# Weights of two attention layers split ahead, parked in DRAM and loaded as parts

## The chip, the cores and the metric

The kernel runs on one core of one Trainium2 chip. The metric is the device time of one execution in microseconds (us), lower is better; a time given is the median of several executions. TensorE (PE) does the matmuls, VectorE (DVE), ScalarE (ACT) and GpSimd (POOL) the elementwise work, SyncE (SP) issues most of the DMAs.

## What is computed

512 tokens of width 1024 pass through two blocks, all in float32. The first block has one layer, the second two. Cut to the calls:

```python
# first block
h = rms_norm(x, mix_norm_g)
u, q, k, v, f_logit, g_ssm, g_att = split(h @ w_in)
y_ssm = s5_branch(u, ...)             # val * sigmoid(gate), [val, gate] = split(gelu(y) @ w_glu)
y_att = forgetting_attention(q, k, v, f_logit, ...)      # 8 heads of 128
x = x + (sigmoid(g_ssm) * y_ssm + sigmoid(g_att) * y_att) @ w_out
x = x + peer_ffn(rms_norm(x), ...)    # product keys: 16 of 16384 experts for each of 8 heads
# second block: an even and an odd attention layer, each followed by a feed-forward
y = rmsnorm(x) @ ev_w_in              # latent, rotary, index and differential parts
x = x + concat([dsa_mixer(...), diff_mixer(...)]) @ ev_w_out    # even: top-128 keys by index scores; differential heads
x = x + (silu(h @ w_gate) * (h @ w_up)) @ w_down
y = rmsnorm(x) @ od_w_in
x = x + nsa_mixer(...) @ od_w_out     # odd: compressed, selected and window branches
x = x + (silu(h @ w_gate) * (h @ w_up)) @ w_down
out = rmsnorm(x)
```

## The kernel before

The stages follow one another: mixer of the first block (0 to about 465 us), its experts (to about 1855), the even attention layer (to 2213), a feed-forward (to 2588), the odd attention layer (to 2995), a second feed-forward and the last norm. Instructions are written in one program order; a scheduler then puts each engine's instructions in an order by when their inputs are ready on its own timeline, so work of neighbouring steps mixes. Each engine and each DMA queue then runs in that fixed order.

Every weight is used in two float32r parts: a product is three matmuls, high by high, high by low and low by high (`mm3`, L332 to L334). The class `Stream` (L57 to L98) makes the parts. All weights stand in one list, `specs`, in the order of their use, cut into units of [128, 1024] (512 KB). `_load` (L66) issues a DMA on SP into a raw tile, `wraw` (three buffers, L68). `_split` (L72) copies the raw tile on ACT into `whi` (L77) and subtracts on DVE into `wlo` (L78); `whi` and `wlo` have three buffers each. `get` (L81) is called where a unit is needed: it splits up to two units further and loads up to three further than that. A unit's `whi` and `wlo` come free when its matmuls have read them. 525 units pass through the stream.

The units differ by where they come from. `add_t` gives units that lie in DRAM as 128 rows of 4 KB; `add_256` gives four pieces of 128 rows of 1 KB (256 columns each); `add_row` two pieces of 512 columns.

The stages that the change touches:
- the gates of the first mixer (L908 to L926): eight steps `g_att`, each a unit and 24 matmuls of 512 columns (`proj_T`), a tanh and a product into `merged`; then eight steps with a unit `glu` (two products, `pv` and `pg`) and a unit `g_ssm`. Before them run the last attention heads and the state-space branch, after them `w_out`.
- the first feed-forward (`ffn` with i = 0, L1220): 22 steps with a unit `gate` and a unit `up`, silu and product, split into `ah` and `al`; then the rows of `down`.
- the even attention layer (`even_mixer`): `ev_a`, `ev_iq`, `ev_qk`, `ev_vb`, `ev_qn`, `ev_out`, 32 units. After the index scores a selection runs as background work on DVE: 16 times `max` and `match_replace` (L1448, L1449) for each of three row tiles, handed out between the differential heads; the latent attention needs its result.
- the odd attention layer (`odd_mixer`): `od_kv`, `od_v`, `od_gc`, `od_k`, `od_q`, `od_out`, 29 units.
- `out_last` (L491) ends each attention layer: the last units are used in pairs (`proj_row`), so that the tiles of tokens end one after the other.

Of the kernel before, what the change touches and what calls it, by code (L numbers as in the profile page):

```python
# [19 lines left out]
P = 128  # L20
T = 512
# [35 lines left out]
class Stream:  # L57
    """Weights in the order of their use: loaded ahead, split ahead into two float32r parts."""
# [22 lines left out]
    def get(self, key, ahead=None):  # L81
# [16 lines left out]
        return self.parts.pop(i)  # L98


def body(ctx, tc, A, out, phases=(1, 2, 3, 4, 5, 6, 7), dumps=None):
# [21 lines left out]
    def banks(**counts):  # L123
        """the eight banks of PSUM, shared out for a phase"""
# [17 lines left out]
    # ---------------------------------------------------------------- weights, in the order of use  # L142
    specs = []

    def add_t(key, ap, n):
        for m in range(n):
            specs.append(((key, m), lambda r: r, ap[m]))

    def add_row(key, ap, c0, w, nk, k0=0):
        for kk in range(k0, nk):  # L150
            specs.append(((key, c0, kk),
                          lambda r, w=w: r[:, :2 * w].rearrange("p (k c) -> p k c", k=2),
                          ap[kk * 256:(kk + 1) * 256, c0:c0 + w].rearrange("(k p) c -> p k c", p=P), 2 * w))

    def add_256(key, ap, c0, nk=KD, k0=0):
        for kk in range(k0 // 4, nk // 4):
            specs.append(((key, c0, kk), lambda r: r.rearrange("p (k c) -> p k c", k=4),
                          ap[kk * 512:(kk + 1) * 512, c0:c0 + 256].rearrange("(k p) c -> p k c", p=P)))

    if 1 in phases:  # L160
        add_t("u", A["w_u"], 4)
        for c in range(8):
            add_256("w_kq", A["w_kq"], 256 * c)
            if c % 2 == 0:
                add_256("w_v", A["w_v"], 128 * c)
        add_t("g_att", A["w_gatt"], 8)
        for m in range(8):
            specs.append((("glu", m), lambda r: r, A["w_glu"][m]))
            specs.append((("g_ssm", m), lambda r: r, A["w_gssm"][m]))
        for c in range(2):  # L170
            add_row("w_out", A["w_out"], 512 * c, 512, 4)

    if 2 in phases:
        add_t("w_query", A["w_query"], 16)
        add_t("peer_u", A["peer_u"], N_SPILL)

        for kind, e, half in peer_order():
            if kind == "u":
                specs.append((("peer_u", e), lambda r: r, A["peer_u"][e]))
            else:  # L180
                specs.append((("peer_v", e, half), lambda r: r.rearrange("p (k c) -> p k c", k=2),
                              A["peer_v"][e * P:(e + 2) * P, half * 512:half * 512 + 512].rearrange(
                                  "(k p) c -> p k c", p=P)))

    def add_ffn(i):
        for m in range(NF):
            specs.append((("gate", i, m), lambda r: r, A["w_gate"][i, m]))
            specs.append((("up", i, m), lambda r: r, A["w_up"][i, m]))
# [3 lines left out]
    if 3 in phases:  # L192
        for c in range(2):
            add_256("ev_a", A["ev_a"], 256 * c)
        for c in range(2):
            add_256("ev_iq", A["ev_iq"], 256 * c)
        for c in range(4):
            add_256("ev_qk", A["ev_qk"], 256 * c)
            if c < 2:
                add_256("ev_vb", A["ev_vb"], 256 * c)  # L200
        add_t("ev_qn", A["ev_qn"], 4)
        for c in range(4):
            add_256("ev_out", A["ev_out"], 256 * c, 8, 4)
        for c in range(2):
            add_row("ev_out", A["ev_out"], 512 * c, 512, 2)
    if 4 in phases:
        add_ffn(0)
    if 5 in phases:
        for c in range(2):
            add_256("od_kv", A["od_kv"], 256 * c)  # L210
        for c in range(2):
            add_256("od_v", A["od_v"], 256 * c)
        specs.append(("od_gc", lambda r: r[:, :384], A["od_gc"], 384))
        for g in range(4):
            if g % 2 == 0:
                add_256("od_k", A["od_k"], 128 * g)
            add_256("od_q", A["od_q"], 256 * g)
        for c in range(4):
            add_256("od_out", A["od_out"], 256 * c, 4)
        for c in range(2):  # L220
            add_row("od_out", A["od_out"], 512 * c, 512, 4, 2)
    if 6 in phases:
        add_ffn(1)
# [1791 lines left out]
```

## Time and profile before

| | us |
|---|---|
| median of three runs | 3382.08 |
| lowest and highest | 3377.85, 3383.44 |
| span of the profiled execution | 3379.4 |
| PE busy in it | 3180.5 |
| DVE busy | 2359.9 |
| ACT busy | 1346.9 |
| POOL busy | 796.8 |

The span is the time from the first to the last instruction of one profiled execution; the profile gives no time beyond it, and it is 2.7 us less than the median. Busy time of PE is modelled from pipelined matmuls: a matmul of 512 columns shows some 0.39 us, while the next one starts 0.23 us later. "Idle before" an instruction is followed by what ended the idle time. A row of the chain says which work ended last at that moment.

### The profile page before, as it was taken

The numbers are of one execution on the slowest core, as the hardware profiler recorded it, in microseconds if no ns is written. First come the engines' busy times: TensorE is split into PE (matmuls) and PEld (weight loads), VectorE is DVE, ScalarE is ACT, GpSimd is POOL, SyncE is SP. The second block draws the span as 40 slices with busy tenths as digits, with TensorE's granted clock in tenths as the row PEclk, the third lists the DMA queues.
The fourth block names the chain that finished last, engine by engine and source line by source line (L and its number), as shares of the span: only waits on it lengthen the run. The fifth ranks groups of instructions, "written<-read, shape, count | busy, mean of one in ns | idle before, by whom it ended". The sixth has DMA issues, their size and how long they took to land.

```text
span 3379.4 us, 47221 instructions
## 1 busy us (share of the span) xinstructions
PE 3180.5 (94%) x17267; PEld 2761.7 (82%) x17267; DVE 2359.9 (70%) x5433; ACT 1346.9 (40%) x2494; POOL 796.8 (24%) x911
## 2 busy tenths in 40 slices
PE   7989999998878899999999996999999998999999
PEld 6988878998877688899997994878887986778887
DVE  6886359999996999889988788743324387753323
ACT  4445233433333333333333454632222377742222
POOL 1451000033354655466774110000000010000000
PEclk9999999999998999999999996999999999999999
DMA  4223232576556999899998321122333210112332
GB/s 141 79 74 111 100 112 88 172 268 208 205 217 214 328 334 320 292 316 348 342 331 303 94 73 41 38 79 96 98 94 131 78 51 1 57 62 94 100 94 81
DMA packets 242809, 529.31 MB, mean 157 GB/s; under 512 B 19080, under 2 KB 113160, under 8 KB 240656
## 3 DMA queue, kind: packets, MB, share of 16 engines
q1 hardware_dynamic: 202832, 376.32, 33.6%
q0 software_dynamic: 36864, 134.23, 11.0%
q10 hardware_dynamic: 2880, 15.73, 1.2%
q8 instruction: 136, 2.23, 0.3%
q14 instruction: 97, 0.79, 0.1%
HBM read 474.17 MB, written 51.40 MB: 156 GB/s over the span
## 4 chain that ended last, share of the span: by engine, by line
PE 56%; DVE 6%; ACT 3%; DMA 2%; issue 2%; POOL 1%; SPq 0%; DVEq 0%; POOLq 0%; ACTq 0%
PE mm L333 15%; PE mm L334 15%; PE mm L332 15%; PE ax L332 2%; PE ax L334 2%; PE ax L333 2%; DVE wlo L78 1%; DMA rw<-in_peer_v_dram,idx 1%; PE tx L1840 1%; PE tx L1280 1%; POOL rw L979 1%; PE sx L1820 1%; PE sx L1818 1%; ACT pd L1823 1%; PE po L1850 0%
## 5 line engine op out<-in xcount | busy, mean ns | idle before, releaser
L78 DVE TENSOR_TENSOR wlo<-wraw,whi 128x1024 fp32r<-128x1024 f32 x525 | 681.4, 1298 | 541.7 <-ACT whi L77 534.0
L77 ACT CAST whi<-wraw 128x1024 fp32r<-128x1024 f32 x525 | 550.8, 1050 | 1097.7 <-PE mm L333 406.4
L332 PE MATMUL mm<-hhi,whi 128*128 128x512 f32 (+1 forms) x1672 | 621.2, 373 | 1.9 <-ACT whi L77 1.8
L334 PE MATMUL mm<-hhi,wlo 128*128 128x512 f32 (+1 forms) x1672 | 618.9, 370 | 1.7 <-DVE wlo L78 1.7
L333 PE MATMUL mm<-hlo,whi 128*128 128x512 f32 (+1 forms) x1672 | 619.4, 371 | 0.0
L332 PE MATMUL mm<-whi,hhi 128*128 128x256 f32 (+1 forms) x1280 | 380.5, 299 | 11.3 <-DVE vl L276 4.5
L333 PE MATMUL mm<-wlo,hhi 128*128 128x256 f32 (+1 forms) x1280 | 379.2, 297 | 0.0
L334 PE MATMUL mm<-whi,hlo 128*128 128x256 f32 (+1 forms) x1280 | 378.7, 298 | 0.2 <-DVE hlo L1867 0.2
L332 PEld LDWEIGHTS mm<-hhi,whi 128*128 128x128 f32 x1672 | 315.9, 189 | 43.7 <-ACT whi L77 2.2
L334 PEld LDWEIGHTS mm<-hhi,wlo 128*128 128x128 f32 x1672 | 314.7, 188 | 43.4 <-DVE wlo L78 2.8
L333 PEld LDWEIGHTS mm<-hlo,whi 128*128 128x128 f32 x1672 | 315.0, 188 | 40.8
L333 PE MATMUL mm<-wlo,wth 128*128 128x512 f32 x768 | 305.3, 398 | 10.6 <-DVE wlo L78 10.6
L334 PE MATMUL mm<-whi,wtl 128*128 128x512 f32 x768 | 304.6, 397 | 0.0
L332 PE MATMUL mm<-whi,wth 128*128 128x512 f32 x768 | 288.6, 396 | 3.4 <-ACT whi L77 3.4
L332 PEld LDWEIGHTS mm<-whi,hhi 128*128 128x128 f32 x1280 | 246.6, 193 | 19.2 <-DVE vl L276 4.7
L979 POOL DMA_INDIRECT rw<-in_peer_rows_dram,idx x128 | 148.6, 1161 | 461.4 <-ACT as L1137 189.0
L333 PEld LDWEIGHTS mm<-wlo,hhi 128*128 128x128 f32 x1280 | 246.5, 193 | 6.0 <-issue 0.2
L334 PEld LDWEIGHTS mm<-whi,hlo 128*128 128x128 f32 x1280 | 245.6, 192 | 6.8 <-DVE hlo L1867 0.4
L979 POOL DMA_INDIRECT rw<-in_peer_v_dram,idx x128 | 179.8, 1405 | 105.4 <-DVE acc L996 80.7
L996 DVE SCALAR_TENSOR_TENSOR acc<-rw,act,acc 128x1024 f32<-128x1024 f32 x127 | 180.2, 1419 | 13.0 <-DMA rw<-in_peer_v_dram,idx 11.4
L988 DVE CUSTOM_DVE_ANT_0 rw<-rw,hrow 128x1024 f32<-128x1024 f32 x128 | 178.9, 1403 | 11.2 <-DMA rw<-in_peer_rows_dram,idx 11.2
L333 PEld LDWEIGHTS mm<-wlo,wth 128*128 128x128 f32 x768 | 145.8, 190 | 46.8 <-DVE wlo L78 15.1
(556 smaller groups left out, 5977.5 us busy)
## 6 DMA issues: line engine op xcount, KB each, us to landing
wraw<-in_peer_u_dram SPq DMA_DIRECT2D x128, 512.0 KB
wraw<-in_peer_v_dram SPq DMA_DIRECT2D x128, 512.0 KB
gt<-gst SPq DMA_DIRECT2D x12, 2048.0 KB
g<-gt SPq DMA_DIRECT2D x32, 768.0 KB
wraw<-in_w_gate_dram SPq DMA_DIRECT2D x44, 512.0 KB
wraw<-in_w_up_dram SPq DMA_DIRECT2D x44, 512.0 KB
wraw<-in_w_down_dram SPq DMA_DIRECT2D x44, 512.0 KB
at<-as ACTq DMA_DIRECT2D x20, 768.0 KB
```

The costliest lines, as they stand in the source:

```text
L77: self.nc.scalar.copy(hi[:, :w], r[:, :w])
L78: self.last = self.nc.vector.tensor_sub(lo[:, :w], r[:, :w], hi[:, :w])
L332: PE.matmul(ps, ah, bh, start=start, stop=False)
L333: PE.matmul(ps, ah, bl, start=False, stop=False)
L334: PE.matmul(ps, al, bh, start=False, stop=stop)
L979: G.indirect_dma_start(out=rw, out_offset=None, in_=A[("peer_rows", "peer_v")[m]], in_offset=bass.IndirectOffsetOnAxis(ap=idx[:, k:k + 1], ...
L988: V.tensor_tensor_reduce(rw, rw, hrow, 1.0, 0.0, op0=ALU.mult, op1=ALU.add, accum_out=act[:, k:k + 1])
L996: V.scalar_tensor_tensor(acc0, rw, act[:, k:k + 1], acc0, op0=ALU.mult, op1=ALU.add)
L1280: K["nc"].tensor.transpose(ps[:, t * P:(t + 1) * P], src(t), K["ident"])
L1818: PE.matmul(ps[:, :N], qr, kh[:, :N], start=True, stop=False)
L1820: PE.matmul(ps[:, :N], qr, kl[:, :N], start=False, stop=True)
L1823: S.activation(p, ps[:, :W], AF.Exp, bias=mx[:, r:r + 1], accum_out=den[:, r:r + 1])
```

## The change

61 units, those of the even and of the odd attention layer, no longer go through the stream's split where they are used. Each gets a tile of [2, 128, 1024] in DRAM (`parked`). Their raw loads and splits stand in the stream at two earlier places: the 32 units of the even layer beside the gates of the first mixer (two behind each `g_att`, two behind each pair of `glu` and `g_ssm`), the 29 of the odd layer behind the steps of the first feed-forward (one or two a step). There `pre` takes the two parts out of the stream and stores them with two DMAs on SP. In the attention layers `_load` does nothing for such a unit, and `_split` issues two DMAs on SP, from DRAM into `whi` and `wlo`. The number of buffers, the distance that the stream runs ahead, the matmuls and all other steps stay. The `phases` switches, the comments and the docstrings are taken out as well. The core of the diff:

```diff
     def _load(self, i):
         view, src = self.specs[i][1:3]
+        if self.specs[i][4] is not None:
+            return
         r = self.pool.tile([P, 1024], F32, tag="wraw", bufs=3, name=f"wraw{i}")
         self.nc.sync.dma_start(view(r), src)
         self.raw[i] = r

     def _split(self, i):
-        r = self.raw.pop(i)
         hi = self.pool.tile([P, 1024], F32R, tag="whi", bufs=3, name=f"whi{i}")
         lo = self.pool.tile([P, 1024], F32R, tag="wlo", bufs=3, name=f"wlo{i}")
-        w = self.specs[i][3] if len(self.specs[i]) > 3 else 1024
+        w, sc = self.specs[i][3:5]
+        if sc is not None:
+            for k, part in enumerate((hi, lo)):
+                self.nc.sync.dma_start(part[:, :w].bitcast(F32), sc[k][:, :w])
+            self.parts[i] = (hi, lo)
+            return
+        r = self.raw.pop(i)
         self.nc.scalar.copy(hi[:, :w], r[:, :w])
         self.last = self.nc.vector.tensor_sub(lo[:, :w], r[:, :w], hi[:, :w])
         self.parts[i] = (hi, lo)
...
+    def pre(self, spec):
+        parts = self.get(("pre", spec[0]))
+        for k, part in enumerate(parts):
+            self.nc.sync.dma_start(spec[4][k][:, :spec[3]], part[:, :spec[3]].bitcast(F32))
...
+    def parked():
+        out = [sp[:4] + (dp.tile([2, P, 1024], F32, name=nm("pre")),) for sp in specs]
+        specs.clear()
+        return out
...
+    def ahead_of(which, i, n):
+        return which[i * len(which) // n:(i + 1) * len(which) // n]
+
+    def add_pre(which, i, n):
+        for key, view, src, w, _ in ahead_of(which, i, n):
+            add(("pre", key), view, src, w)
+
+    def split_ahead(which, i, n):
+        for spec in ahead_of(which, i, n):
+            ws.pre(spec)
...
+    for m in range(8):
+        add(("g_att", m), lambda r: r, A["w_gatt"][m])
+        add_pre(ev, m, 16)
+    for m in range(8):
+        add(("glu", m), lambda r: r, A["w_glu"][m])
+        add(("g_ssm", m), lambda r: r, A["w_gssm"][m])
+        add_pre(ev, 8 + m, 16)
...
     def add_ffn(i):
         for m in range(NF):
+            add(("gate", i, m), lambda r: r, A["w_gate"][i, m])
+            add(("up", i, m), lambda r: r, A["w_up"][i, m])
+            if i == 0:
+                add_pre(od, m, NF)
...
+    specs += ev
+    add_ffn(0)
+    specs += od
+    add_ffn(1)
...
         for m in range(8):
             ps = proj_T(("g_att", m), h)
             th = gp.tile([P, T], F32, tag="tg", bufs=4, name=nm("tg"))
             S.activation(th, ps, AF.Tanh, scale=0.5)
             V.scalar_tensor_tensor(merged[:, m], th, 1.0, merged[:, m], op0=ALU.add, op1=ALU.mult)
+            K["split_ahead"](K["ev"], m, 16)
...
             V.scalar_tensor_tensor(merged[:, m], tg, 0.5, merged[:, m], op0=ALU.mult, op1=ALU.add)
+            K["split_ahead"](K["ev"], 8 + m, 16)
...
             S.copy(ah[:, m], sg)
             V.tensor_sub(al[:, m], sg, ah[:, m])
+            if i == 0:
+                K["split_ahead"](K["od"], m, NF)
```

## Rows read from the trace of the kernel before

**Rows 1.** The page: span, busy time by engine, DMA share in 40 slices.

```profile
span 3379.4 us, 47221 instructions
...
PE 3180.5 (94%) x17267; PEld 2761.7 (82%) x17267; DVE 2359.9 (70%) x5433; ACT 1346.9 (40%) x2494; POOL 796.8 (24%) x911
...
DMA  4223232576556999899998321122333210112332
```

**Rows 2.** The page's costliest groups, the stream's splits: busy us, mean ns, idle before.

```profile
L78 DVE TENSOR_TENSOR wlo<-wraw,whi 128x1024 fp32r<-128x1024 f32 x525 | 681.4, 1298 | 541.7 <-ACT whi L77 534.0
L77 ACT CAST whi<-wraw 128x1024 fp32r<-128x1024 f32 x525 | 550.8, 1050 | 1097.7 <-PE mm L333 406.4
```

**Rows 3.** Timeline of PE and ACT in the gates: start, us, engine, line, idle before.

```profile
271.87 0.40 PE L332 MATMUL mm<-hhi,whi 128*128 128x512 f32 x1
...
343.57 1.05 ACT L77 CAST whi<-wraw 128x1024 fp32r<-128x1024 f32 x1 [4.78 <-PE mm L333]
...
349.04 1.05 ACT L77 CAST whi<-wraw 128x1024 fp32r<-128x1024 f32 x1 [3.92 <-PE mm L333]
...
354.63 1.05 ACT L77 CAST whi<-wraw 128x1024 fp32r<-128x1024 f32 x1 [4.05 <-PE mm L333]
...
426.45 1.04 ACT L77 CAST whi<-wraw 128x1024 fp32r<-128x1024 f32 x1 [3.92 <-PE mm L333]
```

**Rows 4.** Windows in the gates: length, PE, PEld, DVE, ACT, POOL, PEclk, DMA share, GB/s.

```profile
360.00:380.00 20.00, 20.00 (x89) 16.22 (x88) 8.68 (x10) 6.18 (x8) 0.00 (x0) 1.00 0.23 80
380.00:400.00 20.00, 20.00 (x88) 16.26 (x87) 6.91 (x9) 5.77 (x8) 0.00 (x0) 1.00 0.32 106
```

**Rows 5.** Windows, the first feed-forward.

```profile
2226.00:2400.00 174.00, 174.00 (x762) 143.96 (x762) 58.53 (x63) 50.69 (x64) 0.00 (x0) 0.99 0.27 91
```

**Rows 6.** Windows, the even attention layer.

```profile
1880.00:1900.00 20.00, 20.00 (x168) 19.82 (x167) 13.80 (x37) 6.84 (x19) 3.53 (x11) 1.00 0.27 79
1900.00:1920.00 20.00, 20.00 (x167) 19.91 (x167) 15.98 (x23) 9.63 (x16) 5.45 (x8) 1.00 0.28 88
...
2000.00:2020.00 20.00, 20.00 (x114) 17.05 (x113) 17.61 (x47) 10.03 (x28) 2.87 (x4) 1.00 0.29 92
...
2040.00:2060.00 20.00, 11.07 (x43) 7.85 (x41) 16.70 (x56) 10.43 (x33) 0.00 (x0) 0.67 0.08 26
2060.00:2080.00 20.00, 11.66 (x57) 8.96 (x56) 17.70 (x53) 7.74 (x29) 0.00 (x0) 0.67 0.00 1
2080.00:2100.00 20.00, 9.32 (x40) 6.93 (x41) 16.74 (x57) 7.96 (x24) 1.17 (x2) 0.59 0.05 14
```

**Rows 7.** The chain in the attention layers, its pieces of splits: start, us, what.

```profile
1854.59 0.95 ACT whi L77
...
2016.62 1.23 DVE wlo L78
...
2872.71 1.13 DVE wlo L78
```

**Rows 8.** L78 alone, 1960 to 2095: window with DVE busy, and DVE's wait there.

```profile
1960.00:2095.00 135.00, 14.61 (x12) 0.84 0.20 65
...
DVE wlo L78 <- ACT whi L77: 4.0, 5, 1.1
```

**Rows 9.** Windows of 1 us: the end of one load, and two stores.

```profile
354.00:355.00 1.00, 1.00 (x6) 0.82 (x5) 0.00 (x0) 0.37 (x1) 0.00 (x0) 1.00 0.13 49
...
468.00:469.00 1.00, 1.00 (x6) 0.84 (x5) 0.21 (x2) 0.77 (x3) 0.00 (x0) 1.00 1.02 406
469.00:470.00 1.00, 1.00 (x6) 0.80 (x6) 0.83 (x3) 0.44 (x2) 0.00 (x0) 1.00 1.03 414
```

**Rows 10.** The chain in the experts: a 2048 KB store until its source is free.

```profile
1056.87 6.34 DMA gt<-gst
```

**Rows 11.** Timeline of SP's queue: one load in the gates, three stores behind the mixer.

```profile
351.37 0.33 SPq L69 DMA_DIRECT2D wraw<-in_w_gssm_dram  x1
...
467.03 4.70 SPq L470 DMA_DIRECT2D x_sc<-xr  x3
```

More of the change, by code (lines that the diff above doesn't have):

```diff
@@ L143, in body, with add @@
     specs = []
+    def add(key, view, src, w=1024, sc=None):
+        specs.append((key, view, src, w, sc))
     def add_t(key, ap, n):
         for m in range(n):
-            specs.append(((key, m), lambda r: r, ap[m]))
+            add((key, m), lambda r: r, ap[m])
     def add_row(key, ap, c0, w, nk, k0=0):
         for kk in range(k0, nk):
-            specs.append(((key, c0, kk),
-                          lambda r, w=w: r[:, :2 * w].rearrange("p (k c) -> p k c", k=2),
-                          ap[kk * 256:(kk + 1) * 256, c0:c0 + w].rearrange("(k p) c -> p k c", p=P), 2 * w))
+            add((key, c0, kk), lambda r, w=w: r[:, :2 * w].rearrange("p (k c) -> p k c", k=2),
+                ap[kk * 256:(kk + 1) * 256, c0:c0 + w].rearrange("(k p) c -> p k c", p=P), 2 * w)
@@ L155, in add_256 @@
     def add_256(key, ap, c0, nk=KD, k0=0):
         for kk in range(k0 // 4, nk // 4):
[L157 to L183, printed above, removed]
+            add((key, c0, kk), lambda r: r.rearrange("p (k c) -> p k c", k=4),
+                ap[kk * 512:(kk + 1) * 512, c0:c0 + 256].rearrange("(k p) c -> p k c", p=P))
@@ new lines, in parked @@
+    def parked():
+        out = [sp[:4] + (dp.tile([2, P, 1024], F32, name=nm("pre")),) for sp in specs]
+        specs.clear()
+        return out
+    for c in range(2):
+        add_256("ev_a", A["ev_a"], 256 * c)
+    for c in range(2):
+        add_256("ev_iq", A["ev_iq"], 256 * c)
+    for c in range(4):
+        add_256("ev_qk", A["ev_qk"], 256 * c)
+        if c < 2:
+            add_256("ev_vb", A["ev_vb"], 256 * c)
+    add_t("ev_qn", A["ev_qn"], 4)
+    for c in range(4):
+        add_256("ev_out", A["ev_out"], 256 * c, 8, 4)
@@ new lines, in body @@
+    for c in range(2):
+        add_row("ev_out", A["ev_out"], 512 * c, 512, 2)
+    ev = parked()
+    for c in range(2):
+        add_256("od_kv", A["od_kv"], 256 * c)
+    for c in range(2):
+        add_256("od_v", A["od_v"], 256 * c)
+    add("od_gc", lambda r: r[:, :384], A["od_gc"], 384)
+    for g in range(4):
+        if g % 2 == 0:
+            add_256("od_k", A["od_k"], 128 * g)
+        add_256("od_q", A["od_q"], 256 * g)
+    for c in range(4):
+        add_256("od_out", A["od_out"], 256 * c, 4)
@@ new lines, in body @@
+    for c in range(2):
+        add_row("od_out", A["od_out"], 512 * c, 512, 4, 2)
+    od = parked()
+    def ahead_of(which, i, n):
[6 more added lines that the diff above has]
+            ws.pre(spec)
+    add_t("u", A["w_u"], 4)
+    for c in range(8):
+        add_256("w_kq", A["w_kq"], 256 * c)
+        if c % 2 == 0:
+            add_256("w_v", A["w_v"], 128 * c)
@@ new lines, in body @@
+    for m in range(8):
[5 more added lines that the diff above has]
+        add_pre(ev, 8 + m, 16)
+    for c in range(2):
+        add_row("w_out", A["w_out"], 512 * c, 512, 4)
+    add_t("w_query", A["w_query"], 16)
+    add_t("peer_u", A["peer_u"], N_SPILL)
+    for kind, e, half in peer_order():
+        if kind == "u":
+            add(("peer_u", e), lambda r: r, A["peer_u"][e])
+        else:
+            add(("peer_v", e, half), lambda r: r.rearrange("p (k c) -> p k c", k=2),
+                A["peer_v"][e * P:(e + 2) * P, half * 512:half * 512 + 512].rearrange("(k p) c -> p k c", p=P))
@@ L185, in add_ffn @@
     def add_ffn(i):
         for m in range(NF):
-            specs.append((("gate", i, m), lambda r: r, A["w_gate"][i, m]))
-            specs.append((("up", i, m), lambda r: r, A["w_up"][i, m]))
+            add(("gate", i, m), lambda r: r, A["w_gate"][i, m])
+            add(("up", i, m), lambda r: r, A["w_up"][i, m])
+            if i == 0:
+                add_pre(od, m, NF)
         for c in range(2):
             add_row(("down", i), A["w_down"][i], 512 * c, 512, NF // 2)
[L192 to L221, printed above, removed]
```

2 lines of the change are left out of this document (removed).

## The prediction

> **What bounds the kernel now.** I read the page first [rows 1]: PE is busy 94% of 3379.4 us, DVE 70%, and the 16 DMA engines are full only in the middle (the expert stage). The span is 2.7 us under the median of the runs (3382.08), so the sum is made on 3379.4 and 2.7 is added at the end. The two costliest groups of the page are the splits, 525 copies on ACT and 525 subtractions on DVE [rows 2]: 61 of these 525 pairs belong to the units that the change moves (32 `ev_*`, 29 `od_*`). Then the stretches, by the table of windows, because the move takes work from some and gives it to others.
>
> The gates of the first mixer run from the first `g_att` matmul at 271.9 to the last `g_ssm` one at about 426.4 (the split that this releases) [rows 3], 154.5 us. PE is full there, DMA a quarter to a third [rows 4]. One weight unit takes 5.47 us of PE, two take 11.06: the splits start at 343.57, 349.04 and 354.63, each the moment PE ends a unit, since only then one of three `whi`/`wlo` buffers is free [rows 3]. The eight `g_att` (8 x 5.47 = 43.8) and eight pairs `glu`, `g_ssm` (8 x 11.06 = 88.5) make 132.3 of the 154.5; the rest is work of the last heads.
>
> The first feed-forward is PE without a gap, DVE a third busy, DMA 0.27 [rows 5]. In the even layer PE is full until about 2015, and from 2040 to 2100 it is busy half the time at a granted clock of 0.59 to 0.67 (1.2 GHz instead of 2.4 for part of the time) while DVE is busy 51 of 60 us [rows 6]: there DVE with the selection's 48 steps ends last.
>
> **What is removed.** 61 copies and subtractions leave the attention layers. In the even layer the chain of waits goes through 13 such pieces, 13.5 us in all: 2.9 at its entry, 5.7 between 2015 and 2040, 4.8 after 2095; in the odd layer through two, 2.1 us ([rows 7]: the first, one of the middle and the last of the 15). Stretch by stretch:
> - 1960 to 2095: 12 subtractions of 1.22 us, 14.6 us, and 4.0 us in which DVE stood for the copy before them [rows 8]. At most 18.6 us go, if DVE sets the end throughout; at least the 5.7 on the chain, if freed DVE time before 2015 (when PE ends last) is worth nothing. I take 11: the selection steps can move forward into that time, but the heads' own round of scores, maximum and exponent is next late.
> - entry: 0 to 2.9, I take 1.5, because two loads of 512 KB stand where two splits stood. After 2095: 0 to 4.8, I take 3. Odd layer: 0 to 2.1, I take 1.5.
> Together 17 us, between 6 and 28 (28.4 as the plain sum of the upper ends).
>
> **What is added in the gates.** Each parked unit costs a load, a split and two stores of 512 KB. ACT and DVE have room (one split is 1.05 and 1.23 us per unit, and DVE is under half busy there [rows 4]). DMA has less. A load of 512 KB with 4 KB rows: share 0.23 and 0.32 of two 20 us windows at one load per 5.53 us, mean 0.275, so 1.52 us of all engines [rows 4]. One with 1 KB runs, as most `ev_*` have: 524 KB at 79 and 88 GB/s for shares of 0.27 and 0.28, thus 303 GB/s at full share, 1.73 us [rows 6]. A store: `x_sc` at 406 and 414 GB/s for shares of 1.02 and 1.03, 400 at full share, 1.31 us [rows 9, 11]. So
> - a `g_att` with two parked units: 1.52 + 2 x 1.73 + 4 x 1.31 = 10.2 us of DMA, eight are 82;
> - a pair `glu`, `g_ssm` with two: 2 x 1.52 + 2 x 1.73 + 4 x 1.31 = 11.7 us of DMA against 11.06 of PE, eight are 94.
> 176 us, and some 5 for the other traffic of the stretch; less 5 for the three raw tiles loaded ahead and 5 for the last stores, which nobody waits for: 171 against 154.5. At full share of the engines +16 us; at a share of nine tenths, 171 / 0.9 = 190, +35. Full share was held only where many transfers were queued (the expert slices of [rows 1]); here three buffers limit the queue. I take +25.
>
> The Trainium skill, page "DMA: Bandwidth & Descriptors", section "Where 436 GB/s comes from", says that between HBM and SBUF the HBM side, some 358 GB/s for a core, binds before the fabric. The store rows above go over that, so the row decides; by the skill's figure a store would be 1.46 us, the 64 stores would ask 10 us more, not 176 but 186, and the forecast would be near 3406.
>
> **Buffers.** A parked unit keeps its `whi`/`wlo` pair until its stores have landed, which no row of before shows. Near it: a 2048 KB store released its source 6.34 us after the issue [rows 10]; less two quarters at 1.31, about 3.7 us for the 1024 KB here. Split and store are then 6.0 us, split and matmuls 2.3 + 5.5 = 7.8. A pair period has 2 x 7.8 + 2 x 6.0 = 27.6 us of holding over three buffers, 9.2, under 11.06, as long as the stores don't queue. Whether a unit gets the buffer that comes free first or that of the unit three places back cannot be seen, since so far both are the same one. In the second case `glu` m+1 would need the buffer of `g_ssm` m: its split could start only as PE runs dry, up to 2.3 us a period, 13.4 against 11.06, +18 in eight pairs. That is inside the +16 to +35, as the waits overlap.
>
> **In the feed-forward.** 29 parked units over 22 steps: 15 steps take one, 7 take two. DMA is 2 x 1.52 + 4.35 = 7.4 us for one and 11.7 for two, per 10.94 us of PE. On the whole it fits; 7 x 0.8 = 5 us if nothing is evened out. With the buffer of three places back the steps with two stall up to 2.3 each, 16. DVE gets 29 x 1.23 = 36 us more and is a third busy. I take +4, between 0 and 16.
>
> **Part loads.** The attention layers now read 1024 KB for a unit, not 512. A 512 KB load issued at 351.37 has moved its last byte before 355 [rows 9, 11], about 3 us; two are some 4.6, against 2.3 for a split. PE has two units ahead of it, each about as long as those of [rows 3], and DMA is at 0.3 or less [rows 6], so it is covered. It is not covered where two units are held together, in the last rows of both output projections, and at the odd layer's entry, where `x_sc` and the norm's gains stand in the same SP queue: 0 to 8 us, I take +2. Behind a part load that waits for its buffer on SP stand the next loads, and the attention's tables.
>
> **Sum.** 3379.4 + 25 + 4 + 2 - 17 = 3393.4, plus 2.7: 3396. With the ends: 16 + 0 + 0 - 28 = -12 to 35 + 16 + 8 - 6 = +53, 3370 to 3435.
>
> **Rivals.** *Faster: the stores ride along.* If a store's write goes on while reads go on, a period asks 5.0 or 6.5 us of DMA, less than PE, and the gates lose only bubbles, about 3; with 19 us of relief, 2 in the feed-forward and 1 for part loads it is 3382.1 + 3 + 2 + 1 - 19 = 3369. It decides once the gates lose less than 11 us (17 - 4 - 2). For it: stores move faster than loads; 22 us of head work can fill PE's gaps. Against it: during the `x_sc` stores alone the engines are at full share already [rows 9].
> *Much slower: a ring of waits.* Stores, raw loads and the loads behind them share SP's queue. If it is ordered so that a store stands behind a raw load, and that load behind the split that frees its tile, and that split behind the buffer of an earlier store, then two splits and two stores follow each other in a period: 2 x (2.3 + 3.7) + 5.5 = 17.5 us, not 11.06. Eight pairs +52, the `g_att` no less than 2 each, 16, less 11 of net relief: 3382.1 + 57 = 3439. Against it: SP so far waits little, and the order may be better than written.
> *It cancels.* Gates at their low end, +16, with relief 17 and nothing else: 3381.
>
> **How the numbers follow.** Forecast (3389 to 3425) 0.47, the ring of waits (or the relief lost with it) 0.14, cancel 0.13, stores ride along 0.26. A measurement here can tell about 0.2%, 6.8 us: slower 0.61, same 0.13, faster 0.26. For 8 in 10 the range goes from below the faster rival's time to above the forecast's own upper part: 3364 to 3428.
>
> **What would show it.** Right: from about 270 to the end of `g_ssm` some 180 us, not 154.5, DMA share 0.85 to 1.0 there, PE gaps ended by `whi` or by the split's raw load; the feed-forward's steps still 10.9 us each, 11.5 at most where two units are parked; 2015 to 2095 shorter by about 11 with no `wlo` in DVE's rows. Wrong: DMA share in the gates well under 0.85 and PE still full (the stores ride along), SP waits for `wlo` with the DMA engines idle (the ring), or PE waits for part loads in the even layer.

## The result, and the profile after

The changed kernel takes 3411.19 us (median of four, 3409.93 to 3411.72) against 3382.22 for the kernel before (four on the same chip, 3377.85 to 3383.44): the ratio is 1.009, 95% interval 1.0076 to 1.0104. It is 29 us slower, where 14 were forecast. The profiled execution has a span of 3409.9 us, 30.5 more than [rows 1]; the stages below are read from these two.

The page of the changed kernel: span, busy time, DMA share in 40 slices, bytes, and the engines of the chain.

```profile
span 3409.9 us, 47706 instructions
...
PE 3191.4 (94%) x17267; PEld 2762.7 (81%) x17267; DVE 2356.4 (69%) x5433; ACT 1350.2 (40%) x2494; POOL 788.6 (23%) x911
...
DMA  4228962475564999899998541157854430213232
...
HBM read 537.48 MB, written 114.70 MB: 191 GB/s over the span
...
PE 51%; DVE 6%; DMA 6%; ACT 3%; issue 2%; POOL 1%; SPq 0%; DVEq 0%; ACTq 0%; POOLq 0%
```

Two new hills stand in the DMA slices, one at 8 9 6 (the gates), one at 7 8 5 (the first feed-forward), and the chain has DMA at 6%, where it was 2% before; stores of parked parts have 4 of the 6.

Each stage's time against before. The boundaries are the last product into `merged` (431.2 before), the first `xn` of the even norm (1852.4), of the first feed-forward's norm (2213.4) and of the odd norm (2594.1), and the end.

| stage | forecast | measured |
|---|---|---|
| gates | +25 | +23.4 |
| w_out and experts | 0 | +0.1 |
| even layer | -15.5 | -6.4 |
| first feed-forward, to the odd norm's first `xn` | +4, and +2 for part loads | +18.8 |
| odd layer and the rest | -1.5 | -5.4 |
| span | +14 | +30.5 |

**The gates** run with the DMA engines nearly full, as forecast. The windows of the changed kernel from just ahead of the first parked store (264.5) to the last `g_att` product and from there to the last pair's (from:to, length, busy us and instructions of PE, PEld, DVE, ACT and POOL, granted clock, DMA share, GB/s):

```profile
262.00:355.30 93.30, 80.70 (x411) 66.54 (x409) 63.41 (x111) 54.13 (x99) 7.55 (x4) 0.93 0.93 337
355.30:454.50 99.20, 93.96 (x395) 73.39 (x396) 55.93 (x62) 45.52 (x56) 0.00 (x0) 1.00 0.97 353
```

In [rows 4] the DMA share was a quarter to a third. Now it is 0.93 and 0.97: 93.3 x 0.93 = 87 us and 99.2 x 0.97 = 96 us at full share, for which the forecast had 82 and 94. ACT's copies wait there for raw loads more than for stores, as they would where transfers end last (window 355 to 454: us in total, times, longest):

```profile
ACT whi L87 <- DMA wraw<-in_ev_out_dram: 14.4, 7, 3.7
ACT whi L87 <- DMA pre<-whi: 7.9, 5, 2.0
```

**The first feed-forward** does not. Its DMA share is 0.70 to 0.88 in windows of 20 us from 2270 on, and yet PE waits. Waits of the changed kernel from 2245 to 2510 (engine, line, releaser: us in total, times, longest):

```profile
ACT whi L87 <- DMA pre<-whi: 95.8, 27, 6.2
...
PE mm L372 <- DVE wlo L88: 6.9, 10, 1.9
...
SPq L74 <- DVE wlo L88: 148.9, 67, 12.9
```

ACT's copy (L87) stands 95.8 us for stores that must first leave a `whi`; SP's raw loads (L74) stand behind the splits that free a raw tile. How a step with two parked units goes, in the timeline of the changed kernel (start, us, engine, line; in brackets the idle time before and its releaser; L114 is the store, L74 the raw load):

```profile
2279.86 0.45 SPq L114 DMA_DIRECT2D pre<-wlo  x1
...
2281.04 1.05 ACT L87 CAST whi<-wraw 128x1024 fp32r<-128x1024 f32 x1 [2.25 <-DMA pre<-whi]
...
2282.11 0.33 SPq L114 DMA_DIRECT2D pre<-whi  x1
...
2284.12 0.38 SPq L74 DMA_DIRECT2D wraw<-in_od_v_dram  x1
...
2284.55 0.50 SPq L114 DMA_DIRECT2D pre<-wlo  x1
...
2286.57 1.05 ACT L87 CAST whi<-wraw 128x1024 fp32r<-128x1024 f32 x1 [2.45 <-DMA pre<-whi]
2286.66 0.33 SPq L74 DMA_DIRECT2D wraw<-in_w_gate_dram  x1
```

A split waits for a store, the store goes out after the split, the raw load of `gate`, which PE needs next, after that. To have one measure I took the starts of the matmuls of the 44 `gate` and `up` units and of the first `down` unit behind them, which follow each other every 0.227 us where nothing waits, and summed what goes beyond: 0 before, 15.0 us in the changed kernel, 1.8 of them in the `down` unit. The first gap is at 2320, after seven steps; until then PE lives on its lead. The other 3.8 us are at the end: the odd norm's gains come late. DVE's wait for them in the changed kernel, 1.5 us before:

```profile
DVE xn L361 <- DMA grow<-in_norm_mix_dram: 5.5, 1, 5.5
```

**The even layer** gives back less than half of what was forecast. The time from its norm to the first `qr` row, from there to the first score maximum of the differential heads, through the heads' score stages up to the fourth's first maximum ("heads 1 to 3"), and from that maximum to the last head's output ("tail"); and how many of the 48 selection rounds stand ahead of the third head's output scaling in DVE's order:

| kernel | to `qr` | to first maximum | heads 1 to 3 | tail | rounds |
|---|---|---|---|---|---|
| before | 22.3 | 94.6 | 101.5 | 27.5 | 39 |
| changed | 18.6 | 89.9 | 94.3 | 34.9 | 48 |

The first two columns give back 8.4 us, where the forecast had 1.5. The heads give back 7.2, and the tail takes 7.4 again: in the stretch for which 11 were forecast nothing stays. Why can be seen in the changed kernel's timeline (L1490 is a selection round, L304 to L307 the steps of a reciprocal root for the third head, L1551 its scaling):

```profile
2090.78 0.15 DVE L304 TENSOR_TENSOR rt<-ry 128x4 f32<-128x4 f32 x1
...
2093.61 0.16 DVE L305 TENSOR_TENSOR rt<-rt,rv 128x4 f32<-128x4 f32 x1
...
2097.45 1.47 DVE L1490 MAX8 m<-sel 128x8 f32<-128x256 f32 x3
2098.84 0.67 DVE L1551 TENSOR_TENSOR on<-po,ry 128x512 f32<-128x512 f32 x1
...
2099.57 1.11 PE L1322 MATMUL tx<-ident,on 128*128 128x128 f32 x4 [12.13 <-DVE on L1551]
...
2110.99 0.69 DVE L1551 TENSOR_TENSOR on<-po,ry 128x512 f32<-128x512 f32 x1
```

The third head's small steps of 0.15 us stand 2 to 3 us apart with the selection between them; PE stands 12.13 us for that head. The fourth head's transposes stand behind it in PE's order, and so that head's output follows 12 us later, though DVE is out of other work by then.

### The profile page after: what moved, and what is told of

It is laid out like the page before. It is cut to its first block, busy times and chain, and to the rows that moved or that the text cites. A ratio compares the mean times of both kernels' runs of the same rounds, so it can differ in the third digit from the quotient of the medians.

```text
span 3409.9 us, 47706 instructions
## 1 busy us (share of the span) xinstructions
PE 3191.4 (94%) x17267; PEld 2762.7 (81%) x17267; DVE 2356.4 (69%) x5433; ACT 1350.2 (40%) x2494; POOL 788.6 (23%) x911
## 4 chain that ended last, share of the span: by engine, by line
PE 51%; DVE 6%; DMA 6%; ACT 3%; issue 2%; POOL 1%; SPq 0%; DVEq 0%; ACTq 0%; POOLq 0%
PE mm L371 13%; PE mm L372 13%; PE mm L370 13%; DMA pre<-wlo 3%; PE ax L370 2%; PE ax L372 2%; PE ax L371 2%; DVE wlo L88 1%; DMA pre<-whi 1%; PE tx L1882 1%; DMA rw<-in_peer_v_dram,idx 1%; PE tx L1322 1%; PE sx L1862 1%; PE sx L1860 1%; PE po L1892 0%
## 5 line engine op out<-in xcount | busy, mean ns | idle before, releaser
L87 ACT CAST whi<-wraw 128x1024 fp32r<-128x1024 f32 x525 | 549.1, 1049 | 988.9 <-PE mm L371 268.3
L372 PEld LDWEIGHTS mm<-hhi,wlo 128*128 128x128 f32 x1672 | 315.3, 189 | 56.8 <-DVE wlo L88 16.4
L1036 DVE SCALAR_TENSOR_TENSOR acc<-rw,act,acc 128x1024 f32<-128x1024 f32 x127 | 178.6, 1406 | 13.4 <-DMA rw<-in_peer_v_dram,idx 12.9
## 6 DMA issues: line engine op xcount, KB each, us to landing
g<-gt SPq DMA_DIRECT2D x32, 768.0 KB, 10.4
```

The lines of the kernel that those rows point to most:

```text
L87: self.nc.scalar.copy(hi[:, :w], r[:, :w])
L372: PE.matmul(ps, al, bh, start=False, stop=stop)
L1036: V.scalar_tensor_tensor(acc0, rw, act[:, k:k + 1], acc0, op0=ALU.mult, op1=ALU.add)
```

## The experiments

The column names are those of the first table; "gaps" are PE's gaps in the feed-forward as above, all differences to the profiled execution of before.

| run | time, ratio to before | gates | even | feed-forward (gaps) | odd and rest |
|---|---|---|---|---|---|
| changed | 3411.2, 1.0090 | +23.4 | -6.4 | +18.8 (15.0) | -5.4 |
| e1_own_buffers | 3411.3, 1.0089 | +34.3 | -7.2 | +2.2 (1.1) | -5.5 |
| e2_half_stores | 3401.3, 1.0060 | +35.1 | -11.2 | +1.9 (0.1) | -8.7 |
| e3_pool_stores | 3415.3, 1.0105 | +35.5 | -11.1 | +14.8 (10.0) | -7.5 |
| e4_relief_only | 3369.5, 0.9968 | +3.9 | -13.4 | +1.5 (0.0) | -4.2 |
| e5_own_ffn | 3398.5, 1.0050 | +29.6 | -6.5 | +4.1 (2.5) | -3.7 |
| e6_selection_pace2 | 3411.7, 1.0097 | +23.9 | -9.0 | +16.7 (12.5) | -3.6 |
| e7_spread | 3392.6, 1.0039 | +16.7 | -1.9 | +3.5 (0.8) | -8.8 |
| e8_odd_one_a_step | 3403.9, 1.0070 | +23.5 | -5.2 | +4.0 (0.0) | -4.2 |
| e9_half_own | 3396.0, 1.0035 | +20.2 | -6.1 | +3.0 (3.7) | -6.1 |
| e10_pairs12 | 3373.6, 0.9974 | +5.8 | -1.5 | -1.4 (0.0) | -6.0 |
| e11_odd_only | 3375.7, 0.9981 | +0.5 | -0.1 | +0.3 (0.0) | -3.4 |
| e12_late12 | 3374.7, 0.9977 | +1.8 | -5.1 | -0.5 (0.0) | -5.7 |

The rest to the span lies in the experts, where no kernel was changed: -2.8 to +6.8, so a few us between two kernels mean nothing by themselves.

**Buffers of their own.** Parked units take their parts from a second pair of tags; in the gates that pool can open only when the heads' tiles are gone.

```diff
-        hi = self.pool.tile([P, 1024], F32R, tag="whi", bufs=3, name=f"whi{i}")
...
+        own = self.own if self.specs[i][0][0] == "pre" else None
+        pool, tag, nb = (own, "p", 2) if own else (self.pool, "w", 3)
+        hi = pool.tile([P, 1024], F32R, tag=tag + "hi", bufs=nb, name=f"{tag}hi{i}")
...
```

> The parked units get two whi/wlo pairs of their own, in the gates and in the first feed-forward; the other units keep their three. Nothing else differs from the changed kernel. Theory: the gates are set by the DMA engines, the first feed-forward by the three shared buffers. Then the gates' loss stays at 16 to 23 us (23.4 with shared buffers; 16 is what the transfers ask at full share), that of the feed-forward's steps falls from 15.5 to 0 to 4, and the time is about 3396 us (3411 less 12 to 15, less up to 7). Rival 1, buffers set the gates too: the gates' loss falls under 8 and the time is near 3380. Rival 2, the feed-forward is set by slow transfers and not by buffers: it keeps its 15 us, the time stays at 3405 to 3411.

The feed-forward did as the theory said: gaps 1.1 us, not 15.0. All that PE waited for there in this kernel is one row:

```profile
PE mm L374 <- DVE wlo L90: 0.7, 1, 0.7
```

The gates did not get better but 11 us worse, which neither theory had. Its windows from 295, where all parked stores but the first two begin, to the last `g_att` product and from there to the last pair's:

```profile
295.00:367.30 72.30, 55.21 (x214) 41.23 (x213) 43.72 (x65) 39.43 (x60) 0.00 (x0) 0.83 0.96 361
367.30:465.50 98.20, 94.44 (x396) 74.81 (x397) 58.16 (x61) 46.32 (x56) 0.00 (x0) 0.98 0.98 351
```

The share is 0.96 and 0.98: nearly the same transfers, but from 295 on, not from 262. So the shared buffers cost the feed-forward its 15 us. In the pairs buffers of their own gave nothing (98.2 us, 99.2 in the changed kernel), at a share of 0.98: there the DMA engines end last. For the `g_att` this run doesn't tell buffers from transfers, since its own pool opens late and presses the transfers together.

> The changed kernel with two whi/wlo pairs of their own for the parked units in the first feed-forward only; the gates share three as in the change. Theory (three shared buffers cost the feed-forward's steps their 15 us, the DMA engines the gates theirs): the gates keep 23, PE's gaps between the units of the feed-forward go from 15.0 us to 2 or less, as where both had buffers of their own (1.1), the even layer stays as in the changed kernel, and the time is 3411 - 13 = 3398, between 3396 and 3401. Rival (the gaps went there for another reason, a later start or other traffic): 3405 or more.

With the edit in the feed-forward alone the time is 3398.5, 12.7 us under the changed kernel, as expected. (Its profiled execution is the longest of its four, 3408.9 against 3396.2 to 3399.5; of it only the gaps, 2.5, and the stretches of the even layer are used.)

**Which parked units make the gaps.** `parked(lambda i: i < 22)` for the odd units.

> No even unit is parked; of the 29 odd units the first 22 are, one for each step of the first feed-forward, and the last seven are split in the odd layer as before. Buffers and queue are those of the change. Theory (one parked unit in a step fits three buffers, the steps with two cost the 15 us): PE's gaps in the feed-forward are 0 to 3 us, the odd layer gives back 1 to 4 and the time is 3378 to 3384, no change that can be told. Rival (any parked unit makes the ring): gaps of 22/29 of 15, 11 us, time 3389 to 3393.

The text on record is wrong in one point: this kernel parks all 32 even units, as the change does, and is to be held against the changed kernel. The gates show it (+23.5). The gaps are 0.0, though ACT still waits for stores:

```profile
ACT whi L87 <- DMA pre<-whi: 52.6, 21, 4.5
```

One parked unit a step fits three buffers, with slack for a wait of 2.5 us each; the seven steps with two cost 15.0 / 7 = 2.1 us each. The time, 3403.9, is 7.3 us under the changed kernel and not 15: by the profiled executions the feed-forward is 14.8 shorter, but the odd layer, with seven splits back, gives 1.2 less, and the even layer and the experts came out 1.2 and 2.2 longer.

**The queue.** The stores issued by POOL (`nc.gpsimd.dma_start`).

> The stores of the parked parts are issued by POOL's queue instead of SP's; all else as in the changed kernel. Theory (three buffers in the feed-forward, of which a part is the order on SP: stores behind raw loads that wait for splits): the gates keep 18 to 23 us; the feed-forward's 15.5 us fall to 5 to 10, since a store goes out the moment its split ends, but the buffer is still held until it has landed; time 3400 to 3406. Rival 1, the ring of SP's queue is all of it: the feed-forward loses 0 to 3, time about 3397. Rival 2, the queue has no part in it, only the buffers: 15 us stay, time 3409 to 3413. If POOL's queue moves the stores more slowly, the gates lose more than 23.

The gaps fall to 10.0, the upper end of the theory: off SP's queue a third of them goes, and two thirds stay with the buffers. (Two things changed at once: its page has the stores' 63 MB in a queue of the kind software_dynamic, not hardware_dynamic. They landed in 5.2 and 6.9 us in the median, as on SP.) But the gates lose 12 us more, at shares of 0.87 to 0.99, and the time is 3415.3. The Trainium skill ("Trainium Kernel Development and Optimization", section "Key Constraints") says that DMAs from SP, ACT and POOL queues run on the same 16 engines and interleave, and that several queues save issue time only; by that rule the gates could gain nothing, and the trace agrees (+35.5, not +23.4). That they lose it doesn't explain, and no run here does; what shows is that the raw loads of `ev_qk` and `ev_out` landed in 7.9 and 8.2 us in the median, for 6.1 and 6.7 in the changed kernel. Nor are the 5 us of gaps that went in the feed-forward issue time: a store on SP stood behind raw loads, which waited 148.9 us in all for splits (row above).

**Half the bytes.**

```diff
-            self.nc.sync.dma_start(spec[4][k][:, :spec[3]], part[:, :spec[3]].bitcast(F32))
+            self.nc.sync.dma_start(spec[4][k][:, :spec[3] // 2], part[:, :spec[3] // 2].bitcast(F32))
...
```

> Left out: the second half of each parked part is not stored (256 KB for a store, not 512), and the part loads read the first half twice. Number and order of the stores, the buffers and all waits stay as they are. Theory (the DMA engines set the gates): 64 stores at half of 1.31 us take away 42 us of transfers, 171 becomes 129, under the 154.5 us of the gates, so of the 23.4 us lost there at most 5 stay; in the feed-forward the stores land about 1 us sooner and of 15.5 us some 8 stay; the time is about 3411 - 18 - 8 = 3385. Rival (the buffers and the order of the queue set both): the gates keep 12 us or more and the feed-forward 12, the time is 3397 or more.

Both theories missed. The feed-forward's gaps vanished (0.1); a store now lands in 4.3 and 5.3 us in the median, not 5.2 and 6.8. The gates got longer, +35.1, with the engines no longer full. Its window of the pairs and ACT's first wait from 355 to 466:

```profile
352.20:466.30 114.10, 95.67 (x390) 74.12 (x389) 56.11 (x62) 45.34 (x57) 0.00 (x0) 0.95 0.72 235
```

```profile
ACT whi L88 <- DMA pre<-whi: 50.9, 16, 6.9
```

In the changed kernel that wait was 7.9 us in the same steps. With smaller stores the copies on ACT and the subtractions on DVE got another order within a pair, and in that order the buffers bind where the engines did before. So this run doesn't price the transfers; it shows a second limit close behind the first.

> Left out: the second half of each parked part is not stored, and the part loads read the first half twice; the parked units have two whi/wlo pairs of their own in the gates and the first feed-forward. It joins the two edits that each by itself left the gates 34 to 35 us longer. Theory (two limits lie one behind the other in the gates: with whole stores the DMA engines, share 0.96 to 1.04; with half stores the three shared buffers, ACT's split waiting 55.7 us for stores at a share of 0.65 to 0.76): with both taken away the gates lose 0 to 6 us, PE's gaps in the feed-forward are under 2, and the time is 3382 + 4 in the gates - 5 in the even layer + 1 - 2 in the odd = 3380, between 3375 and 3386. Rival (a third limit, the order on SP's queue, in which raw loads stand behind stores): the gates still lose 15 or more, time 3391 or more.

With both edits the gates lose 20.2, not 0 to 6: by the numbers the rival, but not for its reason. The windows of `g_att` and of the pairs:

```profile
295.00:355.20 60.20, 50.39 (x219) 37.67 (x217) 44.62 (x66) 39.78 (x60) 0.00 (x0) 0.91 0.93 308
355.20:451.40 96.20, 91.15 (x387) 73.16 (x387) 57.78 (x63) 46.34 (x57) 0.00 (x0) 0.98 0.90 294
```

The share is still 0.93 and 0.90. Two things were wrong in my sum. A store of half the bytes saves less than half the time. Against e1 the transfers went from 72.3 x 0.96 + 98.2 x 0.98 = 166 us to 60.2 x 0.93 + 96.2 x 0.90 = 143. By the rates in the same rows e1 moved 60.6 MB, of which halving the 62 stores in them would leave 44.3; e9 moved 46.8. So some 7 us of the 143 are 2.5 MB of other loads (an estimate, at 1.52 us for 512 KB). A half store then saves (23 + 7) / 62, about 0.5 us, and not 0.65. And the sum must not be made over the whole of the gates: a `g_att` with two parked units still asks 1.52 + 3.46 + 4 x 0.8 = 8.2 us for 5.47 of PE, and the stream can't shift that to the pairs. 14.4 of the 20.2 are lost in the eight `g_att`, and here too the own pool opens late. 3.8 are lost in the pairs, where the same sum, 9.7 us for 11.06 of PE, has no loss. What costs them, SP's order or another, stays open; so does how much of the gates' 23.4 in the changed kernel would go with the bytes.

**The relief by itself.** One parked pair stands for all, so the attention layers load parts and nothing else is parked.

```diff
+    one = dp.tile([2, P, 1024], F32, name=nm("pre"))
...
-        out = [sp[:4] + (dp.tile([2, P, 1024], F32, name=nm("pre")),) for sp in specs]
+        out = [sp[:4] + (one,) for sp in specs]
...
-        return which[i * len(which) // n:(i + 1) * len(which) // n]
+        return which[:1] if which is ev and i == 0 else []
```

> Left out: the parking, but for the first two units of the gates; one pair of parked parts stands for all, and every part load of the two attention layers reads that pair. So the attention layers run as in the changed kernel, and the gates and the feed-forward as before. It prices the relief alone. Theory, from the changed kernel's stages: the even layer gives back 5 us (4.5 up to the index scores, 3 in the stretch set by DVE, 2.4 lost after it), the odd layer 2 net (5.4 less the 3.4 that its norm's gains come later): 3382 - 7 = 3375, of which 2 are not certain. Rival 1, the relief is the 17 us that were forecast, and was hidden by the later start: 3367 or less. Rival 2, the part loads eat the relief: 3380 to 3386.

The edit parks one unit, where the text on record has two. 3369.5: between the theory and rival 1, and nearer to that. The even layer gives back 13.4 and the odd 4.2, together 17.6, where the prediction had 17. The instructions of the two layers are those of the changed kernel, yet the even layer is 7 us shorter. The even layer's stretches, as in the table above:

| kernel | to `qr` | to first maximum | heads 1 to 3 | tail | rounds |
|---|---|---|---|---|---|
| changed | 18.6 | 89.9 | 94.3 | 34.9 | 48 |
| e1, e5, e8, e9 (from, to) | 18.9, 19.7 | 89.3, 89.9 | 94.2, 94.4 | 33.5, 35.4 | 48 |
| e2 and e3 | 19.6, 19.5 | 89.7, 89.9 | 94.3 | 29.1 | 42 |
| e4 | 18.7 | 89.9 | 93.7 | 28.1 | 39 |
| e6 | 18.8 | 89.9 | 91.3 | 35.6 | 40 |

All agree up to the fourth head's first maximum; then the tail goes with the number of rounds that stand ahead of the third head. From that maximum to the fourth head's scaling, the changed kernel and e4:

```profile
2078.50:2111.00 32.50, 14.60 (x73) 11.78 (x71) 22.05 (x80) 11.94 (x44) 1.16 (x2) 0.66 0.03 9
```

```profile
2059.50:2084.60 25.10, 12.97 (x65) 9.72 (x63) 22.01 (x78) 11.41 (x42) 1.62 (x2) 0.77 0.04 11
```

DVE does 22.05 and 22.01 us of work, in 32.5 and in 25.1 us. So it is not the amount of DVE's work; what differs is its order.

> The changed kernel, in which the even layer gives two steps of the selection to DVE for each stage of a head instead of three; with that the third head's output scaling stands behind 40 of the 48 selection rounds in DVE's order, not behind all 48 (39 before). Theory (the relief of the stretch set by DVE was 4.5 us instead of the 11 forecast because of that order; with 39 rounds the relief was 11.9): the last head's output comes 4 to 7 us sooner than in the changed kernel, time 3404 to 3407. Rival (DVE's work as a whole sets the end, in whatever order): 3409 to 3413.

`yield_bg(3)` became `yield_bg(2)`. The last head's output came 2.3 us sooner (even norm to output -10.4, not -8.1), not 4 to 7, and the time did not move. With the smaller pace the third head stands behind 40 rounds, but only 34 were done at the fourth head's maximum, so 14 were left for the tail, 35.6 us. So the place of the third head's scaling alone is not the cause; what counts is how many rounds stand between the fourth head's maximum and the outputs of the third and fourth. That agrees with all fourteen kernels: with no round between that maximum and the third head's scaling the tail is 26.7 to 28.4 us (six kernels), with three 29.1 (two), with nine 33.5 to 35.4 (five), and e6 has six there. It is still an argument from the order: a kernel in which only DVE's order is swapped was not tried.

**A version that pays.**

> A version that takes the parts of the change that pay: 16 of the 32 even units are parked (the second half of the entry's four loads, and all twelve of the stretch that DVE sets), one for each g_att and one for each pair glu, g_ssm; the odd units in the first feed-forward with two buffer pairs of their own; the odd norm's gains on POOL's queue. DVE's order has the third head behind 39 selection rounds. Theory: a g_att with one asks 1.52 + 1.73 + 2.62 = 5.9 us of DMA for 5.5 of PE, a pair 3.0 + 1.7 + 2.6 = 7.4 for 11.06, so the gates lose 3 to 6; the even layer gives back 9 to 12, the feed-forward loses 1, the odd layer gives back 4 to 7: 3382 + 5 - 10 + 1 - 5 = 3373, between 3367 and 3378. Rival (the gates lose by the order of the queue and the shared buffers and not by transfers): they still lose 12 or more, time 3380 or more.

> Only the twelve even units of the stretch that DVE sets are parked, and only beside the eight pairs glu, g_ssm (one or two for each), none beside g_att; of the odd units the first four, which the odd layer needs at once, stay as before, 25 are parked in the first feed-forward; parked units have two pairs of buffers of their own. Theory (beside g_att the cover of the last heads is lost, 8.5 to 10 us at the first g_att with any parked unit there; beside the pairs one unit costs nothing, as with 16 parked): a pair with 1.5 asks 9.6 us of DMA for 11.06 of PE, the gates lose 0 to 4; the even layer gives back 2 to 8, the feed-forward loses 1, the odd layer gives back 3 to 5: 3382 + 2 - 5 + 1 - 4 = 3376, between 3370 and 3382. Rival (any parked unit in the gates costs, wherever it stands): the gates lose 8 or more, time 3384 or more.

> The same without the even units: only 25 odd units are parked, in the first feed-forward, with two pairs of buffers of their own. Theory: gates and even layer as before the change (within 2), PE's gaps in the feed-forward under 2.5, the odd norm's gains come 0 to 2 us later, the odd layer gives back 4 to 5: 3382 + 1 + 1 - 5 = 3379, between 3376 and 3384, no change that can be told. Rival (the later gains and the part loads eat the odd layer's relief): 3382 to 3386; if the relief is only in the kernels where the layer starts late: 3386 or more.

> As the kernel with twelve even units beside the pairs, but the twelve units are those from the second half of the third head's weights on (three of ev_qk, four ev_qn, five of ev_out). In that kernel 7 of the 10 splits between the first score maximum and the last head's output were still there, because splits run two units ahead of their use: the stretch took 129.1 us there, 129.0 before, 121.8 where all 32 were parked and DVE kept the order of before. Theory: without any of the ten splits, and with DVE's order as before (third head behind 39 selection rounds), the stretch takes 121 to 124 us; gates lose 4 to 7 as there; time 3373.5 - 6 = 3368, between 3364 and 3371. Rival (the gain of the stretch comes only together with the earlier entry, whose splits stay here): the stretch stays at 127 to 130, time 3372 to 3376.

e7 parks one even unit beside each `g_att` and each pair; e10 and e12 park twelve, beside the pairs only; e11 none; e10 to e12 leave the first four odd units as before. The edit of e10 to e12 at the gates:

```diff
     for m in range(8):
         add(("g_att", m), lambda r: r, A["w_gatt"][m])
-        add_pre(ev, m, 16)
...
-        add_pre(ev, 8 + m, 16)
+        add_pre(ev, m, 8)
```

e7 met its rival: the gates lose 16.7 with 16 units. But the pairs, which take one each, lose nothing; 10.2 are lost before the first `g_att` product and 7.1 in the rest of the `g_att`. Windows of e7, the last heads and the pairs; then the pairs of e10 with one or two units each:

```profile
280.00:300.00 20.00, 14.05 (x68) 10.40 (x66) 13.66 (x25) 11.65 (x32) 3.47 (x2) 0.85 0.74 246
...
356.10:447.90 91.80, 89.88 (x391) 72.83 (x390) 45.22 (x52) 34.90 (x46) 0.00 (x0) 1.00 0.67 215
```

```profile
346.00:437.00 91.00, 89.08 (x387) 72.15 (x386) 46.69 (x54) 36.55 (x48) 0.00 (x0) 1.00 0.78 267
```

Between 280 and 300 PE was busy 18.0 us before, with `g_att` matmuls between those of the last heads. As I read it, a parked unit beside `g_att` takes a buffer and a place on ACT from them, so fewer stand ready: 14.05 in e7, 15.3 in the changed kernel, which loses 8.5 of its 23.4 us there. Without units beside `g_att` it is 3.0 (e10) and 0.3 (e12). The pairs themselves take one or two each at a share of 0.78 without getting longer (91.0 us, 92.4 before). They are not quite free: the last `g_att`, by when their first stores are under way, takes 12.5 us in e10 and 12.7 in e12, where it took 8.3.

e10 hit its time, though not as expected: gates +5.8, even layer only -1.5. Of ten splits between the first maximum and the last output seven were still there, since splits run two units ahead of their use. e12 parks the units of those ten: the heads take 95.3 and the tail 26.7, 122.1 in all as expected (129.0 before, 129.1 in e10). The time is 3374.7 all the same, not 3368. Against e10 the even layer as a whole is 3.6 us shorter, as the entry, with all its splits in place, gives 2.5 of it back; and the experts, where nothing was changed, came out 3.9 longer. e11 shows what the odd units give alone: 3375.7, at the lower end of what was expected. The three are 0.2 to 0.3% faster than before (intervals 0.9963 to 0.9984 for e10, 0.9972 to 0.9990 for e11, 0.9968 to 0.9986 for e12) and can't be told from each other.

In e10 and e11 DVE waits 1.4 and 1.7 us for the odd norm's gains, not 5.5. In e7 the gains were on POOL's queue, with the wait at 6.2. So it isn't the queue: the wait goes with the part loads of the first odd units, issued just ahead of the gains. The row of e11:

```profile
DVE xn L365 <- DMA grow<-in_norm_mix_dram: 1.7, 1, 1.7
```

## Why the prediction was right and wrong

**Direction and range** held; the time was 15 us beyond the forecast. The stages say where: the feed-forward with its end is 18.8 for 4 + 2, 12.8 too little, and the relief is 11.8 (6.4 + 5.4) for 17, 5.2 too much; the gates 1.6 the other way. 12.8 + 5.2 - 1.6 = 16.4, the 30.5 of span less 14.

**Gates, +25: right in its step, with luck in the number.** DMA share 0.93 and 0.97 (nine tenths to full was the assumption), no gain in the pairs from more buffers (e1), pairs with one or two units no longer than before (e7, e10). That the loss falls with the bytes is not shown: with half of them (e2, e9) other limits came up. Not seen was that 8.5 of the 23.4 us go before the first `g_att` product, so what is left for the transfers beside `g_att` and pairs is 15. The prediction counted the heads' work as something that fills PE's gaps; it is the `g_att` matmuls that fill the heads' gaps, and parked units take them away.

The prediction weighed the Trainium skill's statement that between HBM and SBUF some 358 GB/s bind ("DMA: Bandwidth & Descriptors", "Where 436 GB/s comes from"). The gates ran at 337 and 353 on the whole, which agrees; but single windows of 20 us held 381 in the changed kernel and 409 in e1 (340 to 360, share 1.04), which doesn't. The Trainium skill, in the section "Measured (HBM→SBUF, 128 partitions, SWDGE, issued from GpSimd)" of the same page, has 425 GB/s for a core while the other core of its pair is idle; 409 stays under that.

**Feed-forward, +4 of 0 to 16: the step that failed.** The prediction named the mechanism (two parked units in a step against three buffers, up to 2.3 us each in seven steps, 16) and left it open; the value taken was the one without it. Measured: 15.0, 2.1 a step; 1.1 with own buffers, 0.0 with one unit a step, 10.0 with the stores on another queue. What argued for the low end was that DMA fits on the whole. It does, at 0.70 to 0.88 in the changed kernel. But a buffer is held from split to landing: the prediction took 3.7 us for two stores, and their medians are 5.2 and 6.8 us.

**Relief, -17: right in sum, not in place, and the change did not get it all.** e4 gave 17.6. The entry, up to the first maximum, gave 8.4 and not 1.5: the chain's 2.9 us of splits [rows 7] were taken for the most that could go, and more went. It goes with the splits there (e12, which leaves them all, has 22.3 and 94.6 as before); that work freed on ACT and DVE off the chain makes up the rest is my reading, not shown. The stretch of the selection gave 7.2 in the heads (11 with [rows 8]), and the tail took it back (7.4), since, by the orders compared above, DVE's order put the selection's rest ahead of the third head. After 2095: forecast -3, measured +1.8. Odd layer: -5.4, not -1.5; no run shows where in it.

**Part loads, +2 of 0 to 8:** the odd norm's gains came 4 us later (5.5 of waiting for 1.5), the place that the prediction named. No wait of PE for a part load is among the rows read in the even layer.

**Rivals.** *The stores ride along* fell: transfers filled the engines. *The ring of waits* was wrong for the gates of this kernel and right as a mechanism: it is what costs the feed-forward 15 us, and the gates of e2. *It cancels* fell with the size of the feed-forward's loss.

## What to carry to other kernels

Before work is moved beside other work, count three things there, each for the single step and not for the stage: the transfers, how long a shared buffer is held until a store has landed, and which matmuls were the cover of somebody else's latency. Where one step in three asks for two and the buffers fit one, the step pays, whatever the mean; spread it to one a step or give it buffers of its own. And relief on an engine is paid out only if the order on that engine lets the work that ends last go first: look at that order in the new kernel, not only at the busy time saved.

## What the runs showed of the hardware that I had not expected

- Loads and stores mixed ran at up to 409 GB/s in a window of 20 us (e1, share 1.04), and 351 to 361 over whole stages.
- Stores of 256 KB in rows of 2 KB saved about 0.5 us each against 512 KB in rows of 4 KB (an estimate from the windows of e1 and e9), less than half of the 1.31 us worked out from [rows 9].
- A store of 512 KB took 5.2 us (`whi`) and 6.8 us (`wlo`) from issue to landing in the median, in the changed kernel, where its bytes ask 1.31 us of the engines by [rows 9].
- A load of a norm's gains let DVE go 7.5 us after its issue (2622.4 to 2630.0) with three part loads issued in the 2 us before it, 4.5 us in the kernel before (2589.6 to 2594.1).
- From the fourth head's maximum to its scaling, the even layer ran at a mean granted clock of 0.66 in the changed kernel and 0.77 in e4, where PE was busy 14.6 of 32.5 and 13.0 of 25.1 us: where PE stood longer, more of the time was at 1.2 instead of 2.4 GHz.
